# Turning the rows of x with a diagonal of 1/rms in the front of a hybrid decoder step

## The chip, the cores and the metric

The kernel runs on one core of a Trainium2 chip. The metric is the device time of one execution in microseconds, lower is better. All engines of the core work from one program: TensorE (PE, with its weight loads PEld), VectorE (DVE), ScalarE (ACT), GpSimd (POOL), and the SP queue, which issues most of the loads.

## What is computed

One layer of a decoder step over 1024 prompt rows and 64 sample rows of width 1024. Only the front of it is touched by the change: the adaLN coefficients, the normalised input h and the first columns of its large product.

```python
def rmsnorm(x, g):
    y = xf * lax.rsqrt(jnp.mean(xf * xf, axis=-1, keepdims=True) + EPS)
    return (y * g)
...
    mod = jax.nn.silu(c) @ w_ada + b_ada
    shift, scale, gate = jnp.split(mod, 3, axis=-1)
    h = rmsnorm(x, norm_g) * (1 + scale[:, None]) + shift[:, None]
    proj = h @ w_in
    u_pool, z_pool, z_ssm, xbc, dt_raw, g_raw = jnp.split(proj, SPLITS, axis=-1)
    ...
    y = (y + d_skip.astype(jnp.float32)[:, None] * xs).reshape(b, L, D_INNER)
```

The pooling branch, the convolution, the state-space scan, the output products and the final norm follow; their code is the same before and after.

## The kernel before

The activations are kept with channels on partitions and the 1088 rows along the free axis. x arrives the other way round, in nine blocks of rows (eight of 128, one of 64), so it is turned on TensorE. Products with h run with both operands split into a high and a low part (three matmuls for one), so each tile of h and of the weights is made twice: a rounded high part on ScalarE, and the rest by a subtraction on VectorE or GpSimd (`split`, L160 and L163, for weights; `h_make`, L307 and L299, for h).

`first()` writes the front out by hand, one call after the other, and `in_line` ties every instruction of each engine to this written order. The steps that matter:

- `x_load`, then `ada_load` (L253) and `w_load` (L852), are issued on the SP queue in the order in which they are wanted. A load that goes into a buffer in use waits on the SP queue for its last reader. `ada_load(2, 4..7)` goes into the buffers of part 1 of w_ada.
- `x_square` sums the squares of a block of rows on ScalarE or VectorE; `x_root` takes the square root on ScalarE; `x_unit` (L209, L215, L213) takes the reciprocal on VectorE and scales the rows in place.
- `x_turn(g3, k)` turns the 128 channels k of one of three groups of blocks (2, 3 and 4 blocks) by transposes (L226) into one PSUM tile, of which there are five in rotation, and copies it to `tf[k]` on VectorE (L232) or ScalarE (L230).
- `ada_mm(part, k)` (L261) multiplies silu(c) with one slice of w_ada; after eight of them `ada_out` copies the sum and `ada_end` turns it (L276) and makes the coefficients `md` (L280, L283) of a few channels. Part 0 serves channels k = 0, 1, part 1 k = 2, 3, part 2 k = 4 to 7.
- `h_make(g3, ks)` makes h of a group of rows, and `products` (L872 to L874) multiplies it with the first two weight tiles. `combine` (L490 to L492, L471) then forms sums of h for a Strassen-like scheme of seven products.
- `late_loads` is a generator: its first part loads conv_w, conv_b, dt_bias and d_skip; its second part spreads d_skip over 16 rows (`dx`, L366), turns conv's coefficients and `dx` on TensorE (L368, L369) and copies them out (L370, L371).
- `gate_mm` and `gate_end` (L838) make the gates' coefficients; then `run(wz, hook)` starts the seven products (L592 to L594), with the remaining weight splits (`first_steps`, L538) and sums between them.

Of the kernel before, what the change touches and what calls it, by code (L numbers as in the profile page):

```python
# [11 lines left out]
ALU = mybir.AluOpType  # L12
# [34 lines left out]
def tile_pool_ssd_step(  # L47
# [48 lines left out]
    def PB():  # L96
        return psB.tile([P, 512], F32, tag="ps", name=nm("ps"))
# [4 lines left out]
    def const(shape, name, dt=F32):  # L102
        return cp.tile(shape, dt, tag=name, name=name)
# [78 lines left out]
    xr = []  # L182
    xbig = [Y4(hs, F32), Y4(hs, F32)]
    ss = const([P, 9], "ss")
    rs = const([P, 9], "rs")
    hh_ = [None] * KT
    hl_ = [None] * KT

# [6 lines left out]
    def x_square(i, eng):  # L195
        xt, n = xr[i]
        sqj = pa.tile([P, D], F32, tag="rawA", name=nm("sqj"), bufs=3)
        if eng is V:
            V.scalar_tensor_tensor(sqj[:n], xt[:n], 1.0, xt[:n], ALU.mult, ALU.mult, accum_out=ss[:n, i:i + 1])
        else:  # L200
            act(sqj[:n], xt[:n], AF.Square, accum_out=ss[:n, i:i + 1])

    def x_root(a, b):
        n = xr[a][1]
        act(rs[:n, a:b], ss[:n, a:b], AF.Sqrt, bias=eps[:n], scale=1.0 / D)

    def x_unit(a, b):
        n = xr[a][1]
        V.reciprocal(rs[:n, a:b], rs[:n, a:b])  # L209
        for i in range(a, b):  # L210
            xt = xr[i][0][:n]
            if i == 6:
                act(xt, xt, AF.Copy, scale=rs[:n, i:i + 1])  # L213
            else:
                V.tensor_scalar(xt, xt, rs[:n, i:i + 1], None, ALU.mult)  # L215

    tf = [None] * KT

    def x_turn(g3, k, eng=None):
        if g3 == 0:  # L220
            tf[k] = tfp.tile([P, T], F32, tag="tf", name=nm("tf"), bufs=8)
        px = PB()
        c = 0
        for i in range((0, *XG)[g3], XG[g3]):
            xt, n = xr[i]
            nc.tensor.transpose(px[:, c:c + n], xt[:n, k * P:(k + 1) * P], ident[:n, :n])  # L226
            c += n
        o = BLK[g3][0]
        if eng is not V and (eng or k % 2):
            act(tf[k][:, o:o + c], px[:, :c], AF.Copy)  # L230
        else:
            V.tensor_copy(tf[k][:, o:o + c], px[:, :c])  # L232


    PARTS = ((0, 2), (2, 4), (4, 8))
# [120 lines left out]
    def late_loads():  # L356
        va = sm.tile([120, P], F32, tag="stc", name="va", bufs=4)
        load(va[0:96, :], conv_w[0].rearrange("k (m p) -> (k m) p", p=P))
        load(va[96:120, :], conv_b[0].rearrange("(m p) -> m p", p=P))
        V.memset(dtb, 0.0)  # L360
        load(dtb[0:NH, 0:1], dt_bias[0].rearrange("(h o) -> h o", o=1))
        dk = sm.tile([16, 2], F32, tag="rsm", name="dk")
        load(dk, d_skip[0].rearrange("(m h) -> m h", h=2))
        yield
        dx = sm.tile([16, 2, 64], F32, tag="stc", name="dx", bufs=4)
        V.tensor_copy(dx, dk.unsqueeze(2).to_broadcast([16, 2, 64]))  # L366
        ps = PB()
        nc.tensor.transpose(ps[:, :120], va, ident[:120, :120])  # L368
        nc.tensor.transpose(ps[:, 120:136], dx.rearrange("m h r -> m (h r)"), ident[:16, :16])  # L369
        V.tensor_copy(cvT, ps[:, :120])  # L370
        V.tensor_copy(Dv, ps[:, 120:136])  # L371
# [471 lines left out]
    def first():  # L843
# [56 lines left out]
        x_root(0, 2)  # L900
        x_unit(0, 2)
        x_square(2, None)
        x_square(3, None)
        x_root(2, 4)
        for k in range(4):
            x_turn(0, k, V)
        x_unit(2, 4)
        x_square(4, None)
        x_root(4, 5)
        for k in range(4, 8):  # L910
            x_turn(0, k)
# [56 lines left out]
        for k in range(4):  # L968
            ada_mm(2, k)
        products(2, range(2, 3))  # L970
        for k in range(4, 8):
            ada_mm(2, k)
        mr = ada_out(2)
        products(2, range(3, 4))
# [957 lines left out]
```

## Time and profile before

| what | value |
| --- | --- |
| median of the runs | 1312.61 us (1308.47, 1312.61, 1314.85) |
| the profiled execution | 1307.32 us, span 1305.6 us, granted clock 0.992 |
| PE / PEld busy | 1260.7 / 1164.8 us (97% / 89% of the span) |
| DVE, ACT, POOL busy | 887.2, 700.6, 677.9 us (68%, 54%, 52%) |
| chain that ended last | PE 79%, DVE 6%, DMA 6%, ACT 3%, issue 3%, POOL 2% |

The span runs from the first to the last instruction of the profiled execution; its own time has 1.7 us around that. A row of the timeline gives start and duration in us, engine, line, operation, output and inputs, how many alike follow each other (x), and in brackets how long the engine was idle before and what ended that. Matmuls are pipelined, so a row's duration includes the last one's drain. A row of the table by stage gives the stretch, its length, the busy time of PE, PEld, DVE, ACT and POOL with the number of instructions, the granted TensorE clock, the DMA engines' share and GB/s; asked for one line's instructions on one engine, it has only that engine's column. Lines such as L226 are those of the kernel before; in the changed kernel the same statements stand some ten lines lower.

### The profile page before, as it was taken

To read this page: it belongs to the slowest core of one execution; us is meant where nothing else is said; L and a number is where in the kernel's file an instruction comes from. 1 tells how busy PE (TensorE), PEld (TensorE's weight loads), DVE (VectorE), ACT (ScalarE), POOL (GpSimd) and SP (SyncE) were. 2 spreads that over 40 slices of the span, in tenths; PEclk is the share of its full clock that TensorE was granted. 3 is DMA by queue.
4 is the path that set the end of the run, shared out by engine and by line. 5 is a ranking of instruction groups with operands and counts; after the bars stand their busy time and mean duration, and the time that the engine had idled before them with its cause. 6 is when DMAs were issued, how large, how long until landed. Compare 5 with 4: busy or idle time off the path is not lost.

```text
span 1305.6 us, 26257 instructions
## 1 busy us (share of the span) xinstructions
PE 1260.7 (97%) x9667; PEld 1164.8 (89%) x9667; DVE 887.2 (68%) x1510; ACT 700.6 (54%) x1662; POOL 677.9 (52%) x562
## 2 busy tenths in 40 slices
PE   6889999999999999999999999999999999999998
PEld 4669999989999999999889999988888888999786
DVE  5677579966979587675657665487565877466533
ACT  6655347366557655555554554677887766201211
POOL 1005668678879777664344353366686756214000
PEclk9989999999999999999999999999999999999999
DMA  9726444465456453443546455999998665474621
GB/s 322 259 97 194 132 163 159 133 204 176 150 162 217 143 181 127 157 149 113 165 142 204 149 174 167 339 355 360 325 278 277 203 202 162 174 260 158 228 103 51
DMA packets 233794, 251.68 MB, mean 193 GB/s; under 512 B 31266, under 2 KB 177906, under 8 KB 233659
## 3 DMA queue, kind: packets, MB, share of 16 engines
q1 hardware_dynamic: 161568, 171.60, 41.0%
q10 hardware_dynamic: 72098, 78.41, 17.6%
q8 instruction: 77, 1.26, 0.4%
q14 instruction: 51, 0.41, 0.1%
HBM read 167.06 MB, written 83.01 MB: 192 GB/s over the span
## 4 chain that ended last, share of the span: by engine, by line
PE 79%; DVE 6%; DMA 6%; ACT 3%; issue 3%; POOL 2%; ACTq 0%; SPq 0%; DVEq 0%; POOLq 0%
PE ps L592 8%; PE mm L592 7%; PE ps L593 7%; PE ps L594 7%; PE mm L594 7%; PE mm L593 7%; PE mm L344 5%; PE mm L345 4%; PE mm L346 4%; PE ps L1878 2%; PE ps L1879 2%; PE ps L1880 2%; PE ps L1204 2%; PE ps L1420 1%; PE ps L1207 1%
## 5 line engine op out<-in xcount | busy, mean ns | idle before, releaser
L163 POOL TENSOR_TENSOR wlo<-rawA,whi 128x512 fp32r<-128x512 f32 x120 | 187.0, 1563 | 198.2 <-ACT whi L160 104.6
L163 POOL TENSOR_TENSOR wlo<-raw,whi 128x512 fp32r<-128x512 f32 x92 | 149.8, 1635 | 122.0 <-ACT whi L160 118.3
L344 PE MATMUL mm<-Y,whi 128*128 128x352 f32 (+1 forms) x480 | 164.0, 342 | 0.6 <-DVE G L1781 0.5
L345 PE MATMUL mm<-Y,whi 128*128 128x352 f32 (+1 forms) x480 | 158.1, 329 | 1.0 <-DVE Y L1455 1.0
L346 PE MATMUL mm<-Y,wlo 128*128 128x352 f32 (+1 forms) x480 | 157.5, 328 | 0.0
L594 PE MATMUL mm<-Y,wlo 128*128 128x272 f32 x496 | 144.1, 291 | 4.9 <-POOL wlo L163 4.4
L592 PE MATMUL mm<-Y,whi 128*128 128x272 f32 x496 | 146.9, 296 | 0.8 <-ACT whi L160 0.8
L592 PE MATMUL ps<-Y,whi 128*128 128x272 f32 x496 | 145.0, 292 | 2.1 <-ACT o L792 1.5
L593 PE MATMUL ps<-Y,whi 128*128 128x272 f32 x496 | 143.6, 290 | 0.0
L593 PE MATMUL mm<-Y,whi 128*128 128x272 f32 x496 | 143.4, 289 | 0.0
L594 PE MATMUL ps<-Y,wlo 128*128 128x272 f32 x496 | 143.1, 289 | 0.0
L160 ACT ACTIVATE whi<-rawA 128x512 fp32r<-128x512 f32 x125 | 78.2, 626 | 98.8 <-PE ps L593 45.5
L1047 DVE SCALAR_TENSOR_TENSOR GA<-GA,cvT,GA 128x1112 f32<-128x1112 f32 x72 | 127.1, 1769 | 1.8 <-ACT GA L1044 1.7
L160 ACT ACTIVATE whi<-raw 128x512 fp32r<-128x512 f32 x96 | 58.9, 626 | 90.0 <-DVE raw L538 39.0
L594 PEld LDWEIGHTS mm<-Y,wlo 128*128 128x128 f32 x496 | 94.0, 189 | 6.7 <-POOL wlo L163 5.7
L592 PEld LDWEIGHTS ps<-Y,whi 128*128 128x128 f32 x496 | 93.8, 189 | 3.8 <-ACT o L792 1.7
L344 PEld LDWEIGHTS mm<-Y,whi 128*128 128x128 f32 x480 | 90.7, 189 | 6.7 <-issue 3.9
L592 PEld LDWEIGHTS mm<-Y,whi 128*128 128x128 f32 x496 | 93.9, 189 | 2.6 <-ACT whi L160 1.0
L593 PEld LDWEIGHTS mm<-Y,whi 128*128 128x128 f32 x496 | 94.0, 189 | 0.7 <-issue 0.6
L593 PEld LDWEIGHTS ps<-Y,whi 128*128 128x128 f32 x496 | 93.9, 189 | 0.3 <-issue 0.2
L594 PEld LDWEIGHTS ps<-Y,wlo 128*128 128x128 f32 x496 | 93.9, 189 | 0.2 <-issue 0.2
L345 PEld LDWEIGHTS mm<-Y,whi 128*128 128x128 f32 x480 | 90.8, 189 | 1.7 <-DVE Y L1455 1.6
(446 smaller groups left out, 3778.7 us busy)
## 6 DMA issues: line engine op xcount, KB each, us to landing
rawA<-in_w_in SPq DMA_DIRECT2D x46, 512.0 KB
dec<-acs_d SPq DMA_DIRECT2D x32, 512.0 KB
xbc<-GA ACTq DMA_DIRECT2D x24, 512.0 KB
xb<-xbc SPq DMA_DIRECT2D x32, 384.0 KB
rawA<-in_w_in SPq DMA_DIRECT2D x32, 256.0 KB
pw<-in_w_ssm_out ACTq DMA_DIRECT2D x32, 256.0 KB
ws<-ph ACTq DMA_DIRECT2D x32, 256.0 KB
ws<-pw SPq DMA_DIRECT2D x32, 256.0 KB
```

The lines of the kernel that those rows point to most:

```text
L160: ins = act(hi[:, :, :ncols], raw[:, :, :ncols], AF.Copy)
L163: (eng or nc.gpsimd).tensor_tensor(lo[:, :, :ncols], raw[:, :, :ncols], hi[:, :, :ncols].bitcast(F32), ALU.subtract)
L344: mm(ps[:, :n], a, rh[k][:, o:o + n], start=(k == 0), stop=False)
L345: mm(ps[:, :n], a, rl[k][:, o:o + n], start=False, stop=False)
L346: mm(ps[:, :n], b, rh[k][:, o:o + n], start=False, stop=(k == nk - 1))
L592: mm(p, hi, ah, start=(k == 0), stop=False)
L593: mm(p, hi, al, start=False, stop=False)
L594: mm(p, lo, ah, start=False, stop=(k == 3))
L1047: V.scalar_tensor_tensor(d[:, :n], rp[:, k:k + n], cvT[:, 24 * k + mc:24 * k + mc + 1], d[:, :n], ALU.mult, ALU.add)
L1204: mm(o[hh], xd[:S, 2 * q + hh, :], dec[:S, 2 * q + hh], start=True, stop=state is None)
L1878: mm(ps[:, :cw], mhk, wo[k][0][:, s], start=(k == 0), stop=False)
L1879: mm(ps[:, :cw], mhk, wo[k][1][:, s], start=False, stop=False)
```

## The change

- `x_unit` no longer scales the rows. It builds, for every block of rows, a 128x128 diagonal matrix of 1/rms from the identity, in a tile `dg`. `x_turn` multiplies the raw rows with this diagonal in place of the transpose, which turns and scales at once.
- `x_turn` is split: the copy out of PSUM is a call of its own, `x_copy`, so that it can stand elsewhere in the written order; `x_turns` does both in a row, odd k on ScalarE, even k on VectorE.
- In `first()` the squares, roots and turns are written in another order: the squares of blocks 3 and 5 go from ScalarE to VectorE; roots and reciprocals are taken for blocks 2 to 4 and 5 to 8 together, in place of one to three at a time; four columns of the third group are turned ahead of the coefficient products of part 0; the last two columns are turned right behind the transposes of `ada_end(0)`, and their copies stand behind the first `products`.
- Four of the eight `ada_mm(1, k)` move from behind `products(1, ...)` and `h_make(2, ...)` to ahead of `products(1, ...)`.
- In `late_loads` a `yield` divides the second part: `dx` is made right after `combine` is set up, and the turning of conv's coefficients and `dx` comes after `gate_end`.
- `ss` is filled with ones at the start, since the root of blocks 5 to 8 now reads 128 rows of a block that has 64.

The order of the instructions that follow `first()` is the same on every engine.

```diff
     def x_unit(a, b):
         n = xr[a][1]
         V.reciprocal(rs[:n, a:b], rs[:n, a:b])
+        if not dg:
+            dg.append(R())
         for i in range(a, b):
-            xt = xr[i][0][:n]
-            if i == 6:
-                act(xt, xt, AF.Copy, scale=rs[:n, i:i + 1])
-            else:
-                V.tensor_scalar(xt, xt, rs[:n, i:i + 1], None, ALU.mult)
+            n = xr[i][1]
+            V.tensor_scalar(dg[0][:n, i * P:i * P + n], ident[:n, :n], rs[:n, i:i + 1], None, ALU.mult)
...
         for i in range((0, *XG)[g3], XG[g3]):
             xt, n = xr[i]
-            nc.tensor.transpose(px[:, c:c + n], xt[:n, k * P:(k + 1) * P], ident[:n, :n])
+            mm(px[:, c:c + n], xt[:n, k * P:(k + 1) * P], dg[0][:n, i * P:i * P + n], start=True, stop=True)
             c += n
+        return g3, k, px, c
+
+    def x_copy(turned, eng):
+        g3, k, px, c = turned
         o = BLK[g3][0]
-        if eng is not V and (eng or k % 2):
+        if eng is V:
+            V.tensor_copy(tf[k][:, o:o + c], px[:, :c])
+        else:
             act(tf[k][:, o:o + c], px[:, :c], AF.Copy)
-        else:
-            V.tensor_copy(tf[k][:, o:o + c], px[:, :c])
+
+    def x_turns(g3, ks):
+        for k in ks:
+            x_copy(x_turn(g3, k), nc.scalar if k % 2 else V)
...
         V.tensor_copy(dx, dk.unsqueeze(2).to_broadcast([16, 2, 64]))
+        yield
         ps = PB()
...
         x_unit(0, 2)
         x_square(2, None)
-        x_square(3, None)
-        x_root(2, 4)
-        for k in range(4):
-            x_turn(0, k, V)
-        x_unit(2, 4)
+        x_square(3, V)
+        x_turns(0, range(2))
         x_square(4, None)
-        x_root(4, 5)
-        for k in range(4, 8):
-            x_turn(0, k)
-        x_unit(4, 5)
-        x_square(5, None)
+        x_turns(0, range(2, 4))
+        x_root(2, 5)
+        x_unit(2, 5)
+        x_turns(0, range(4, 8))
+        x_square(5, V)
         x_square(6, None)
-        for k in range(4):
-            x_turn(1, k)
+        x_turns(1, range(4))
         x_square(7, V)
-        x_root(5, 8)
-        x_unit(5, 8)
         x_square(8, None)
-        x_root(8, 9)
-        for k in range(4, 8):
-            x_turn(1, k)
-        x_unit(8, 9)
+        x_turns(1, range(4, 6))
+        x_root(5, 9)
+        x_unit(5, 9)
+        x_turns(1, range(6, 8))
         v_turn()
-        for k in range(4):
+        x_turns(2, range(4))
+        for k in range(6):
             ada_mm(0, k)
-        x_turn(2, 0)
-        x_turn(2, 1)
-        ada_mm(0, 4)
-        ada_mm(0, 5)
+        x_turns(2, range(4, 5))
         w_split(0, 0)
         w_split(1, 0)
-        x_turn(2, 2)
-        x_turn(2, 3)
         ada_mm(0, 6)
         ada_mm(0, 7)
         mr = ada_out(0)
-        x_turn(2, 4, nc.scalar)
-        x_turn(2, 5, nc.scalar)
+        x_turns(2, range(5, 6))
         ada_end(0, mr)
+        turned = [x_turn(2, k) for k in (6, 7)]
         h_make(0, range(2))
         products(0, range(2))
-        x_turn(2, 6)
-        x_turn(2, 7)
+        x_copy(turned[0], V)
+        x_copy(turned[1], nc.scalar)
         h_make(1, range(2))
+        for k in range(4):
+            ada_mm(1, k)
         products(1, range(2))
         h_make(2, range(2))
-        for k in range(KT):
+        for k in range(4, KT):
             ada_mm(1, k)
...
         sums = combine()
+        next(late)
         for bi in range(3):
...
             gate_mm(k)
+        gate_end(bg)
         next(late, None)
-        gate_end(bg)
```

More of the change, by code (lines that the diff above doesn't have):

```diff
@@ L184, in tile_pool_ssd_step @@
     ss = const([P, 9], "ss")
+    nc.gpsimd.memset(ss, 1.0)
     rs = const([P, 9], "rs")
+    dg = []
     hh_ = [None] * KT
@@ L209, in x_unit, with x_turn @@
         V.reciprocal(rs[:n, a:b], rs[:n, a:b])
+        if not dg:
+            dg.append(R())
         for i in range(a, b):
-            xt = xr[i][0][:n]
-            if i == 6:
-                act(xt, xt, AF.Copy, scale=rs[:n, i:i + 1])
-            else:
-                V.tensor_scalar(xt, xt, rs[:n, i:i + 1], None, ALU.mult)
+            n = xr[i][1]
+            V.tensor_scalar(dg[0][:n, i * P:i * P + n], ident[:n, :n], rs[:n, i:i + 1], None, ALU.mult)
     tf = [None] * KT
-    def x_turn(g3, k, eng=None):
+    def x_turn(g3, k):
         if g3 == 0:
@@ L970, in first @@
         products(2, range(2, 3))
-        for k in range(4, 8):
+        for k in range(4, KT):
             ada_mm(2, k)
```

## The prediction

> **What bounds the kernel now.** I read the page first (busy shares, the slices), then tables by stage of the first 125 us, where every edited line runs, then the instructions of that stretch in order of time, one engine after the other, and last the rows near the end that already show the two new operations. The last stretch of the table by stage covers the rest.
>
> ```profile
> PE   6889999999999999999999999999999999999998
> ...
> 125.00:1305.00 1180.00, 1157.87 (x8805) 1079.79 (x8803) 804.68 (x1338) 626.05 (x1525) 656.89 (x520) 1.00 0.58 191
> ```
>
> The first number after the stretch's length is TensorE: from 125 us on it is busy 1157.87 of 1180 us. On every engine the written order of the instructions behind the edited stretch is the same before and after. So what the front wins, TensorE starts earlier with, and I let it pass to the end whole. In the first three slices TensorE is at 6 to 8 tenths; the edit lives in these holes.
>
> ```profile
> 9.62 3.67 PE L226 MATMUL ps<-ident,Y 128*128 128x128 f32 x16 [0.19 <-DVE Y L215]
> 21.05 1.08 PE L261 MATMUL ps<-Y,scT 128*32 128x128 f32 x32 [1.59 <-issue]
> 27.36 0.33 PE L276 MATMUL ps<-ident,mr 128*128 128x128 f32 x1
> 28.89 0.38 PE L872 MATMUL mm<-Y,whi 128*128 128x256 f32 x1 [1.20 <-ACT Y L307]
> 31.09 0.49 PE L226 MATMUL ps<-ident,Y 128*128 128x128 f32 x3
> 31.51 0.27 PE L226 MATMUL ps<-ident,R 64*128 64x64 f32 x1
> 31.71 0.55 PE L226 MATMUL ps<-ident,Y 128*128 128x128 f32 x3
> 33.69 0.45 PE L872 MATMUL mm<-Y,whi 128*128 128x384 f32 x1 [1.23 <-ACT Y L307]
> 37.67 2.56 PE L261 MATMUL ps<-G,scT 128*32 128x128 f32 x64
> 80.86 0.32 PE L368 MATMUL ps<-ident,va 120*128 120x120 f32 x1
> 84.76 0.29 PE L369 MATMUL ps<-ident,dx 16*128 16x16 f32 x1 [3.58 <-DVE dx L366]
> 84.98 0.60 PE L592 MATMUL mm<-Y,whi 128*128 128x272 f32 x1
> ...
> 90.41 0.29 PE L592 MATMUL mm<-G,whi 128*128 128x272 f32 x1
> 90.54 0.29 PE L593 MATMUL mm<-G,whi 128*128 128x272 f32 x1
> ```
>
> The bracket is the hole ahead of the row and who ended it. Three kinds stand here: waits in the turns of x; two waits of 1.2 us for the first rows of h (L872); and one of 3.58 us for a 16x128 copy (L366), behind which the first large product (L592) is queued.
>
> **Turning x by a product.** The row for a product of 32-bit 128x128 with a diagonal is in the trace, with the scaling of the identity that makes the diagonal:
>
> ```profile
> L226 PE MATMUL ps<-ident,Y x64: 270/421/476, 9.0 to 32.0; 128*128 128x128 f32 x64
> ...
> 15.00:18.20 3.20, 3.20 (x16) 1.00 1.09 262
> 18.45:19.10 0.65, 0.65 (x7) 1.00 1.09 344
> ...
> 1148.21 0.87 DVE L1734 TENSOR_SCALAR dg<-ident,rs 128x128 f32<-128x128 f32 x4
> 1153.41 1.05 PE L1735 MATMUL ps<-dg,ones 128*128 128x128 f32 x8
> ...
> 7.95 0.17 DVE L209 RECIPROCAL rs<-rs 128x2 f32<-128x2 f32 x1 [0.20 <-ACT rs L205]
> 8.15 1.42 DVE L215 TENSOR_SCALAR Y<-Y,rs 128x1024 f32<-128x1024 f32 x2
> ```
>
> The first row gives the shortest, median and longest time of one transpose in ns, the next two count the transposes (L226 alone) in two stretches. The 8 matmuls of L1735 are 4 calls: a product takes two passes. Leaving off the 0.27 us of the last one, a pass starts every (1.05 - 0.27)/7 = 0.11 us, so a product costs 0.22. A transpose is (0.49 - 0.27)/2 = 0.11 us at 31.09, and (3.67 - 0.42)/15 = 0.217 at 9.62, with the median 0.42 for the last. TensorE runs at half pace there: 16 transposes in 3.2 us from 15.0 on, 7 in 0.65 us after 18.45 (the clock column shows 1.00 for both; so early I go by the counts). So a product costs two transposes: 0.22 at full pace; at half pace no row shows it, and I take twice the half-pace transpose, 0.43. A chunk of 64 rows costs 0.20 (31.51 to 31.71) and becomes about 0.4.
>
> VectorE loses eight scalings of 0.7 us (L215) and ScalarE one; VectorE gets nine diagonals of 0.2 us (L1734: 0.87/4) and two squares more. TensorE can start when the reciprocal and one diagonal are done, 8.15 + 0.28 = 8.4, not 9.0, and then has no scaling to wait for: the 1.59 us at 21.05 (a copy out of PSUM queued behind scalings) goes. It runs without a break, so it should reach full pace after 3.4 to 6.9 us of work (before, the unbroken run from 15 on reached it at 18.4; the 3.7 us from 9.62 did not). Counting with the earlier one: 8 products at 0.43 to 11.9; 32 more of the first 40 at 0.22 to 18.9; 0.2 for L152; four columns of the third group (each 3 x 0.22 + 0.4) to 23.4; six steps of L261 at 0.27 (1.08/4) to 25.0; one column, two steps, one column to 27.7. That is where L276 now stands: 27.7 against 27.36, **+0.3**, and +2 with the late rise of pace. The copies moved between VectorE and ScalarE go at nothing: the lost scalings, some 5 us on VectorE, cover them; a copy without cover would cost TensorE about 0.4 to 0.6 us. The halves w_split makes move behind two copies on ScalarE; GpSimd's part has 1.5 us of room before L873 uses it:
>
> ```profile
> 24.75 2.50 POOL L163 TENSOR_TENSOR wlo<-raw,whi 128x512 fp32r<-128x512 f32 x2 [21.37 <-ACT whi L160]
> ```
>
> **Work put in the waits for h.** From 27.36 to the end of the coefficient products of part 1 (37.67 + 2.56 = 40.23) TensorE takes 12.9 us. After the change the last two columns of x (2.1 us as products) fill the 1.20 us ahead of 28.89, and four of the eight L261 steps (half of 2.56) fill the 1.23 us ahead of 33.69. What is left is work, the products with h at the pace of these two rows (0.17 us for 384 columns, so some 0.12 for 256):
>
> ```profile
> 45.16 0.34 PE L872 MATMUL mm<-Y,whi 128*128 128x384 f32 x1
> 45.33 0.34 PE L873 MATMUL mm<-Y,wlo 128*128 128x384 f32 x1
> ```
>
> 0.3 + 2.1 + 12 x 0.12 + 1.3 + 12 x 0.17 + 1.3 = 8.5 us. So part 1 ends at 27.7 + 8.5 = 36.2, **-4.0**.
>
> That does two things. First, the SP queue waits for exactly these steps, since part 2's last four loads reuse their buffers:
>
> ```profile
> 38.81 2.84 SPq L253 DMA_DIRECT2D G<-in_w_ada x4
> ...
> 36.00:39.00 3.00, 3.00 (x34) 2.47 (x36) 1.93 (x7) 1.75 (x3) 0.00 (x0) 0.50 0.23 64
> 39.00:41.50 2.50, 2.50 (x51) 2.17 (x44) 0.00 (x0) 0.28 (x1) 0.00 (x0) 1.00 0.65 192
> 41.50:47.50 6.00, 5.47 (x32) 4.50 (x30) 4.19 (x13) 3.72 (x7) 0.00 (x0) 1.00 1.05 325
> ```
>
> The last two columns are the DMA engines' share and GB/s: 0.23 and 0.65 before the loads arrive, full after. The hole is worth 0.77 x 3 + 0.35 x 2.5 = 3.2 us. With the first two loads free to go at about 32 and the last two by 36, I take 2.6 us of it as filled; the bounds are 0 and 3.2. Second, that hole decides what comes next:
>
> ```profile
> 51.75 0.69 DVE L538 TENSOR_TENSOR raw<-rawA,rawA 128x512 f32<-128x512 f32 x1 [0.73 <-DMA rawA<-in_w_in]
> ...
> 54.60 0.20 DVE L280 TENSOR_TENSOR md<-ps,vT 128x36 f32<-128x36 f32 x1 [1.43 <-PE ps L276]
> ```
>
> L538 waits for a load and the last coefficients (54.60) are queued behind it on VectorE. TensorE, 4 us ahead, no longer ends that wait; the load does: 51.75 - 2.6 = 49.1, plus L538 and the step behind it, 54.60 - 51.75 - 1.43 = 1.4, gives 50.6, **-4.0** for everything behind L280. Bounds: -1.4 (hole not filled) and -4.6. If TensorE is further ahead than VectorE there, it idles longer and may lose pace again; 0.5 us for that.
>
> **d_skip's rows.** L366 moves ahead of the sums of columns, so that its 16x128 copy is long done when TensorE reaches L369; it costs VectorE 0.21 us earlier. The 3.58 us wait goes whole. Next late would be the first weights; VectorE makes their low half just ahead of the row at 81.29:
>
> ```profile
> 81.29 0.69 DVE L538 TENSOR_TENSOR rawA<-raw,rawA 128x512 f32<-128x512 f32 x1
> 81.95 2.63 DVE L471 TENSOR_TENSOR Y<-tf,Y 128x544 fp32r<-128x544 f32 x4
> 84.50 0.21 DVE L366 COPY dx<-dk 16x128 f32<-16x128 f32 x1
> 85.36 0.41 DVE L838 TENSOR_TENSOR bg<-ps,bg 128x256 f32<-128x256 f32 x1
> 91.56 0.69 DVE L163 TENSOR_TENSOR wlo<-rawA,whi 128x512 fp32r<-128x512 f32 x1 [5.78 <-ACT whi L160]
> ...
> 85.00:90.70 5.70, 5.70 (x28) 5.70 (x28) 0.69 (x3) 0.48 (x2) 0.00 (x0) 0.55 0.06 13
> 91.50:114.40 22.90, 21.67 (x169) 21.01 (x167) 21.16 (x35) 14.59 (x30) 5.69 (x4) 1.00 0.38 119
> ```
>
> So L592 can start at 81.2 - 4.0 + 0.5 = 77.7 instead of 84.98. The clock column also says 0.55 behind the wait: the first 24 matmuls of L592 to L594 took 90.41 - 84.98 = 5.4 us, though at 90.41 the next starts after 0.13. Without the hole they take 24 x 0.13 = 3.1 and end at 80.8, 9.6 us earlier. That ending is what VectorE waited 5.78 us for (L163 behind ScalarE's L160, itself behind the copy of this product). VectorE's own list ends at 85.36 + 0.41 - 4.0 = 81.8, a little after, so its resumption at 91.56 becomes about 82.0: **-9.5**. From there to 114.4 VectorE is busy 21.16 of 22.90 us and sets the pace, so TensorE, now further ahead, wins nothing more; it will show small waits for it there.
>
> The Trainium skill ("TensorE: Matmul & The Clock Gate", Part 1) says one idle window of some 3.4 us halves the clock and a busy one restores it; by that the hole that I expect ahead of L280 (up to 3 us) would cost a whole window at half pace, 1.7 us instead of 0.5, and the sum would be -8.3. The trace is stricter than the rule: 0.55 behind the hole of 3.58 us, but also 0.50 from 36 to 39, behind one of 1.23 us and smaller ones.
>
> **Sum.** The +0.3 at L276 is in the -4.0 behind L280; then +0.5 for pace, -3.8 for the wait (84.98 to 81.2), -2.3 for the pace behind it, and 0.1 back for VectorE's list: -9.5. The profiled execution took 1307.32 us (span 1305.6 and 1.7 around it), so 1297.8 on its scale; it lies 5.3 below the median of the runs shown, 1312.61, and the forecast is set against that: 1312.61 - 9.5 = **1303.1**.
>
> **The rivals.**
> (a) VectorE takes the second half back: the DMA hole's gain arrives, but VectorE, or ScalarE's L160 in front of it, is late anyway, so only -4 to -6 is left: 1307.5. For it: from 81.29 to 84.7 VectorE's rows follow without a hole. Against: 5.78 us idle in the row of 91.56.
> (b) The loads do not move (SP issues them no earlier, or the DMA hole stays): the front gives about -1, d_skip's rows -6: 1306. Against it: the loads wait for L261 alone.
> (c) Slower: the product costs four transposes, not two, and the pace does not rise in the front. Deciding place: L276. Break-even is where the front's loss equals the rest of the gain, 9.5/60 = 0.16 us more per product than 0.22, that is 0.38. At 0.43 throughout (two passes at half pace) it is 60 x 0.21 = 12.6 less 9.8: +3, 1316. At four passes and half pace, 0.86, it is some 60 x 0.64 = 38 less 10: +28, 1341. Against: L1735 shows two passes, and the pace rose in the transposes. The Trainium skill (same page, Terms) calls transpose mode four times faster for 32-bit data, which speaks against this change: by it a product is 0.44 at full pace, 60 x 0.22 = 13 us lost, +3.5 in all. The trace's ratio is 2 (0.22 against 0.11).
> (d) It doesn't do what it says: the order inside the front is as written, but every piece is covered, since the DMA engines set the front all along: 1312. For it: full in 41.5 to 47.5. Against: 3.2 us of hole ahead of that.
>
> **How the numbers follow.** Forecast 0.60; (a) 0.14; (b) 0.08; (c) 0.12; (d) 0.06. The forecast's own bounds are -5.7 (DMA hole not filled, and 1.7 us of lost pace) and -10.6 (hole filled whole, no pace lost), 1302 to 1307; the runs shown spread some 3 us to either side, so 1299 to 1310. With (a) and (b), which 0.82 of the chance needs, the range is 1298 to 1311. Half a per cent (6.6 us) is about what a measurement of this kernel can tell from no change. Faster by more: 0.58 of the forecast's 0.60, 0.06 of (a), 0.04 of (b): 0.68. Within it: what is left of these, and (d): 0.20. Slower by more: (c), which I don't split, 0.12.
>
> **What would show it.** Right: L276 near 27 to 28; no hole ahead of L872's first rows over 0.5 us; the four L253 issues near 32 to 36; L280 near 50.6; no hole at L369, and a clock of 1.00 in the first product; VectorE's L163 near 82; the dense stretch of VectorE ending near 105 instead of 114.4. Wrong: two passes of over 0.25 us, L538 still at 51.7, or VectorE's hole of 5.78 us still open.

## The result, and the profile after

The changed kernel took 1299.05 us (median of 5 runs, 1296.04 to 1301.33) beside 1312.61 us for the kernel before (5 runs, 1308.47 to 1314.85): ratio 0.9902, 95% interval 0.9877 to 0.9928. Run again beside more runs of before, it took 1298.94 us (12 runs) against 1308.62 (28 runs): 0.9931, interval 0.9907 to 0.9954, or 9.0 us (6.0 to 12.2). It is faster. Here and below a gain in us is worked out from the ratio, which is estimated over all runs and is not quite the quotient of the two medians. The profiled execution took 1298.25 us, span 1296.5, against 1307.32 and 1305.6: 9.1 us less.

The stages of the profile after, in the order of the prediction. First TensorE's rows in order of time (start, duration, engine, line, operation, count, idle time before); lines stand some ten lower than before:

```profile
9.69 10.57 PE L228 MATMUL ps<-R,Y 128*128 128x128 f32 x80 [2.00 <-DVE R L216]
...
20.39 0.94 PE L228 MATMUL ps<-R,Y 128*128 128x128 f32 x6
21.25 0.43 PE L228 MATMUL ps<-R,R 64*128 64x64 f32 x2
21.61 0.94 PE L228 MATMUL ps<-R,Y 128*128 128x128 f32 x6
...
29.77 0.33 PE L286 MATMUL ps<-ident,mr 128*128 128x128 f32 x1
...
37.20 1.08 PE L271 MATMUL ps<-G,scT 128*32 128x128 f32 x32
...
79.16 0.23 PE L380 MATMUL ps<-ident,dx 16*128 16x16 f32 x1
79.32 0.40 PE L603 MATMUL mm<-Y,whi 128*128 128x272 f32 x1
...
82.46 0.29 PE L603 MATMUL mm<-G,whi 128*128 128x272 f32 x1
```

The turns of x run on without a hole; L286 (L276 before, at 27.36) is later by 2.4 us. The last coefficient products of part 1 end at 37.20 + 1.08 = 38.28, where they ended at 40.23. The hole of 3.58 us ahead of d_skip's rows is gone, and the first large product takes 82.46 - 79.32 = 3.1 us where it took 5.4. The counts of L228 alone in three stretches (length, TensorE busy with the number of matmuls), then all engines by stage (PE, PEld, DVE, ACT, POOL, clock, DMA share, GB/s):

```profile
9.69:12.60 2.91, 2.91 (x13) 1.00 1.03 411
13.00:16.00 3.00, 3.00 (x30) 1.00 1.06 262
...
30.00:36.00 6.00, 6.00 (x67) 5.29 (x67) 4.36 (x12) 4.55 (x8) 0.00 (x0) 1.00 1.06 351
36.00:41.50 5.50, 5.50 (x55) 4.30 (x53) 2.77 (x11) 3.16 (x7) 0.00 (x0) 1.00 1.00 326
41.50:53.00 11.50, 10.58 (x101) 7.41 (x100) 7.56 (x19) 5.66 (x10) 0.00 (x0) 1.00 0.98 321
84.00:105.50 21.50, 20.77 (x162) 20.12 (x161) 19.87 (x35) 13.74 (x28) 5.00 (x4) 1.00 0.40 126
125.00:1296.00 1171.00, 1149.12 (x8740) 1071.52 (x8738) 803.64 (x1330) 621.93 (x1516) 649.68 (x516) 1.00 0.59 190
```

13 passes in 2.91 us (0.22 each) and then 30 in 3.00: the pace rises at about 12.6, where it had not risen before 18.4. The loads run through from 30 to 53 (shares 0.98 to 1.06), and the half pace behind 36 us is gone. Then VectorE, the SP queue and ScalarE:

```profile
34.61 4.18 SPq L263 DMA_DIRECT2D G<-in_w_ada  x4
...
48.99 0.69 DVE L549 TENSOR_TENSOR raw<-rawA,rawA 128x512 f32<-128x512 f32 x1
...
52.65 0.20 DVE L290 TENSOR_TENSOR md<-ps,vT 128x36 f32<-128x36 f32 x1 [2.24 <-PE ps L286]
...
78.20 0.72 DVE L497 TENSOR_TENSOR Y<-tf,Y 128x544 fp32r<-128x544 f32 x1 [1.21 <-ACT Y L504]
...
84.00 0.68 DVE L163 TENSOR_TENSOR wlo<-rawA,whi 128x512 fp32r<-128x512 f32 x1
...
75.59 0.48 ACT L736 ACTIVATE dts<-mm,dtb 128x256 f32<-128x256 f32 x1 [1.33 <-DMA gs<-g]
```

The load behind L549 is there in time; md is now ended by TensorE (2.24 us), at 52.65 for 54.60. L163 starts at 84.00 without a wait, for 91.56 with one of 5.78. The two waits at 75 to 78 are new in size: ScalarE (L736) waits for the store gs<-g of the gates, 1.33 us for 0.15 before, and VectorE behind it, 1.21 for 0.50.

### The profile page after: what moved, and what is told of

Read it like the earlier page. It is cut to its first block, busy times and chain, and to the rows that moved or that the text cites. A ratio compares the mean times of both kernels' runs of the same rounds, so it can differ in the third digit from the quotient of the medians.

```text
span 1296.5 us, 26406 instructions
## 1 busy us (share of the span) xinstructions
PE 1261.6 (97%) x9739; PEld 1168.5 (90%) x9739; DVE 887.8 (68%) x1512; ACT 696.2 (54%) x1656; POOL 675.4 (52%) x563
## 3 DMA queue, kind: packets, MB, share of 16 engines
q8 instruction: 77, 1.26, 0.4%
## 5 line engine op out<-in xcount | busy, mean ns | idle before, releaser
L163 POOL TENSOR_TENSOR wlo<-rawA,whi 128x512 fp32r<-128x512 f32 x120 | 185.3, 1549 | 188.1 <-ACT whi L160 101.7
L163 POOL TENSOR_TENSOR wlo<-raw,whi 128x512 fp32r<-128x512 f32 x92 | 151.1, 1650 | 121.9 <-ACT whi L160 112.8
L603 PE MATMUL mm<-Y,whi 128*128 128x272 f32 x496 | 146.4, 295 | 0.2
L603 PE MATMUL ps<-Y,whi 128*128 128x272 f32 x496 | 144.4, 291 | 1.4 <-ACT o L803 1.4
L354 PEld LDWEIGHTS mm<-Y,whi 128*128 128x128 f32 x480 | 90.2, 188 | 6.9 <-issue 4.3
L603 PEld LDWEIGHTS ps<-Y,whi 128*128 128x128 f32 x496 | 93.3, 188 | 2.7 <-ACT o L803 1.6
L603 PEld LDWEIGHTS mm<-Y,whi 128*128 128x128 f32 x496 | 93.3, 188 | 2.3 <-issue 0.8
L604 PEld LDWEIGHTS mm<-Y,whi 128*128 128x128 f32 x496 | 93.4, 188 | 0.7 <-issue 0.6
L1196 ACT ACTIVATE dec<-dec,acT 128x128 f32<-128x128 f32 (+1 forms) x288 | 86.7, 383 | 10.0 <-POOL dec L1187 6.3
```

Of the source, the lines that this page charges most:

```text
L163: (eng or nc.gpsimd).tensor_tensor(lo[:, :, :ncols], raw[:, :, :ncols], hi[:, :, :ncols].bitcast(F32), ALU.subtract)
L354: mm(ps[:, :n], a, rh[k][:, o:o + n], start=(k == 0), stop=False)
L603: mm(p, hi, ah, start=(k == 0), stop=False)
L604: mm(p, hi, al, start=False, stop=False)
L1196: act(dec[:, h], dec[:, h], AF.Exp, bias=acT[:S, c, 8 * g + h:8 * g + h + 1], scale=-1.0)
```

## The experiments

### The two parts apart: d_skip's rows, and the front

d_skip alone, on the kernel before:

```diff
         V.tensor_copy(dx, dk.unsqueeze(2).to_broadcast([16, 2, 64]))
+        yield
...
         sums = combine()
+        next(late)
...
-        next(late, None)
         gate_end(bg)
+        next(late, None)
```

> The kernel before with only one part of the change: the step that turns d_skip's rows is cut in two, its VectorE copy runs ahead of the loop over the gate's products and its two transposes come after them, behind gate_end. Front of the kernel untouched. Theory A (the two terms of 53 to 92 us stand by themselves): md stays at 54.6, the second transpose no longer waits 3.58 us for VectorE, so that the products of L592 start at about 81.4 instead of 84.98; with no hole there is no window of half pace, the first product takes 3.1 us instead of 5.4, the first L163 starts near 85.7 instead of 91.56, and the kernel is 5 to 6 us faster (ratio about 0.9955). Theory B (VectorE takes it back, since it is dense from 91.5 to 114.4): L592 starts at 81.4 but VectorE's last step of that stretch moves by less than 2 us, gain 0 to 2 us.

The front alone is the changed kernel with these three places put back.

> The changed kernel with that one part undone: d_skip's rows stand where they stood before, the products with diagonals and the new order of the front stay. Theory A: md starts at 52.6 as in the changed kernel (1.95 us ahead of before), the hole of about 3.6 us before the second transpose and the window of half pace behind it are back, the first L163 starts near 89.6, and the kernel is 2 us faster than before (1.5 to 3 with the even pace of the front). Theory B (the front carries most of the gain, since the pace rises earlier for good): 5 us or more faster.

Measured: d_skip alone 1304.37 us beside 1309.08 (10 and 31 runs), ratio 0.9972 (0.9952 to 0.9991), 3.7 us; the front alone 1305.9, ratio 0.9965 (0.9944 to 0.9987), 4.6 us. Together 8.3, beside 9.0 for the whole: they add up, as far as intervals of 1.2 to 6.3 and 1.7 to 7.3 us can tell. TensorE's and VectorE's rows of d_skip alone, and its stages:

```profile
84.03 0.23 PE L370 MATMUL ps<-ident,dx 16*128 16x16 f32 x1
84.19 0.40 PE L593 MATMUL mm<-Y,whi 128*128 128x272 f32 x1
```

```profile
88.47 0.69 DVE L163 TENSOR_TENSOR wlo<-rawA,whi 128x512 fp32r<-128x512 f32 x1 [1.32 <-ACT whi L160]
```

```profile
27.40:56.00 28.60, 24.93 (x215) 18.98 (x213) 14.55 (x38) 13.72 (x25) 0.40 (x2) 0.88 0.84 280
84.10:91.00 6.90, 6.90 (x55) 6.87 (x56) 5.58 (x12) 5.29 (x10) 0.00 (x0) 1.00 0.09 24
```

The wait and the half pace behind it are gone, as theory A has it (55 matmuls in 6.9 us at clock 1.00, where before had 34 in 6.5 at 0.60). But its front, which is the same code as before, stood at a clock of 0.88 from 27 to 56, where the profiled execution of before had 0.94, and md came at 56.01, not 54.60. From md to L163 it takes 32.46 us, where before took 36.96: 4.5 us won, of the 5 to 6 expected. In that stretch stands a window at half pace, 60.0 to 63.4 (clock 0.50), which the profiled execution of before does not have. The timed 3.7 us (1.2 to 6.3) lies between the two theories and decides neither. The front alone:

```profile
53.50 0.20 DVE L290 TENSOR_TENSOR md<-ps,vT 128x36 f32<-128x36 f32 x1 [2.25 <-PE ps L286]
...
79.59 0.73 DVE L496 TENSOR_TENSOR Y<-tf,Y 128x544 fp32r<-128x544 f32 x1 [1.87 <-ACT Y L503]
...
91.38 0.69 DVE L163 TENSOR_TENSOR wlo<-rawA,whi 128x512 fp32r<-128x512 f32 x1 [5.34 <-ACT whi L160]
```

In this trace md is 1.1 us ahead of the profiled before, 2.5 ahead of the trace above, and 1.4 us is lost again on the wait for gs (1.87 where before had 0.50), so that L163 stands where it stood. The trace thus gives less than the timed 4.6 us (1.7 to 7.3); the time lies between the two theories and decides neither.

### Half pace: filling the holes of before with idle work

```diff
         nc.tensor.transpose(ps[:, :120], va, ident[:120, :120])
+        for _ in range(30):
+            nc.tensor.transpose(ps[:, 136:264], ident, ident)
         nc.tensor.transpose(ps[:, 120:136], dx.rearrange("m h r -> m (h r)"), ident[:16, :16])
```

> The kernel before with 30 extra transposes of the identity, into columns that nobody reads, between the two transposes of d_skip's step: TensorE's hole of 3.58 us before the second one is filled with about 30 x 0.11 = 3.3 us of idle work, and nothing is moved. It leaves the wait where it was and takes away only the idle. Theory A (the half pace of 83.35 to 90.18 comes from the hole): the clock stays at 1.00 through 83 to 92, the first product takes 3.1 us instead of 5.4, L592 still starts near 85, the first L163 near 89.3, the kernel is 2 us faster. Theory B (the pace falls for another reason, the load itself): the clock shows 0.5 again, no gain, or a loss of up to 0.5.

TensorE's rows of it in order of time, and the stage behind them:

```profile
83.20 3.44 PE L370 MATMUL ps<-ident 128*128 128x128 f32 x30
86.64 0.23 PE L371 MATMUL ps<-ident,dx 16*128 16x16 f32 x1
86.80 0.40 PE L594 MATMUL mm<-Y,whi 128*128 128x272 f32 x1
```

```profile
86.80:92.00 5.20, 5.20 (x42) 5.20 (x42) 1.61 (x5) 2.26 (x5) 0.00 (x0) 1.00 0.05 11
```

42 matmuls in 5.2 us at 1.00, behind the same wait: the half pace there comes from the hole, and is worth the 2.3 us of the prediction (the first 24 take 3.1 us, 86.80 to 89.94, where they took 5.4). The other traces agree: a half-paced window follows in all four that have this hole (3.17 to 4.94 us long), and in none of the nine that do not. In time it is 0.9996 (0.9972 to 1.0020), which holds both the 2 us (0.9985) and nothing: the runs scatter by more than this term (1302.99 to 1315.78 us). So the next one puts idle transposes at four holes of the front, on the kernel before, and leaves this one open:

```diff
+        if g3 == 1 and k == 0:                       # x_turn, ahead of the transposes
+            for _ in range(9):
+                nc.tensor.transpose(px[:, 384:512], ident, ident)
...
+            if part == 0:                            # ada_mm, ahead of the first product
+                for _ in range(12):
+                    nc.tensor.transpose(pm[part][:, 256:384], ident, ident)
...
+        if part != 1:                                # ada_end, behind its transposes
+            for _ in range(8):
+                nc.tensor.transpose(pm[part][:, 256:384], ident, ident)
```

> The kernel before with its front's holes filled by idle transposes of the identity: 9 ahead of the second group of rows (hole of 1.05 us), 12 ahead of the first coefficient product (1.59), 8 each ahead of the first products of L872 (1.20) and of the last set (1.26). Nothing moved, the hole of 3.58 us before d_skip's rows left in. Theory A (before's half-paced windows at 20 to 60 us come from these holes, so that they fall otherwise in every execution): no half pace between the rise and 80 us, mean granted clock about 0.992 to 0.993 against before's 0.989, md at 53.5 to 55, the kernel 2 to 3 us faster than before. Theory B (other cause): windows as before, no gain, or up to 1.5 us slower for the idle work.

1307.81 us beside 1308.77 (12 and 17 runs), ratio 0.9983 (0.9964 to 1.0001), 2.2 us with an interval that reaches nothing. The mean granted clock of its runs is 0.993, before's 0.989. Its rows show that two of the four holes stayed open:

```profile
14.77 2.62 PE L229 MATMUL ps<-ident,Y 128*128 128x128 f32 x22 [1.06 <-DVE Y L215]
...
20.06 1.53 PE L265 MATMUL ps<-ident 128*128 128x128 f32 x12 [2.49 <-DVE tf L235]
```

The nine idle transposes ran at 12.34, ahead of two transposes of x that were not late, and the hole came behind these. The twelve waited for VectorE's copy out of PSUM (L235) themselves, and their 1.5 us came on top of that wait. The other two holes shrank, from 1.20 to 0.33 us and from 1.26 to 0.38. md came at 54.97, for 54.60 before. So the run does not tell what filling the whole front is worth. No half pace followed the hole of 2.49 us; one window was left, behind a hole of 1.23 us at the second L872 that had no filler. The stage with that hole, and the window behind it:

```profile
27.70:35.80 8.10, 5.66 (x35) 4.29 (x35) 3.77 (x10) 4.71 (x9) 0.19 (x1) 1.00 1.02 346
35.80:39.30 3.50, 3.50 (x33) 2.98 (x35) 2.52 (x9) 1.75 (x3) 0.00 (x0) 0.51 0.06 15
```

### Four coefficient products moved, alone

```diff
+        for k in range(4):
+            ada_mm(1, k)
         products(1, range(2))
         h_make(2, range(2))
-        for k in range(KT):
+        for k in range(4, KT):
             ada_mm(1, k)
```

> The kernel before with only four of the eight coefficient products of the second set moved ahead of products(1), so that the sync queue's four loads of L253 are issued at 32 to 36 us instead of 38.81. Theory A (the hole of 3.2 us in the loads sets part of the front): the transfers run through 35 to 39, md starts 1 to 2 us ahead of 54.60, the kernel is 1 to 2 us faster. Theory B (the loads are hidden, TensorE's order sets md): the transfers move, md does not move by more than 0.3, no change in time. Theory C (as the prediction had it, the loads and the hole are the larger part of 4 us): md 3 us or more earlier.

Measured: 1307.43 us (10 runs), ratio 0.9988 (0.9969 to 1.0006), and a trace that cannot decide: TensorE was at half pace from 21.5 to 38.5 us, L276 came at 30.65, md at 57.51, and SP's loads at 38.81 as before, though 3.3 us nearer to L276. A stage of it:

```profile
31.00:38.50 7.50, 6.18 (x37) 4.82 (x40) 2.33 (x7) 2.66 (x6) 0.00 (x0) 0.50 0.81 271
```

### The changed kernel once more, its late start, and its order without the product

> The changed kernel itself, timed beside the three kernels below. Before's front showed half-paced windows at other places in each of the last executions, the changed kernel's none up to 613 us. Theory A (a good part of the gain is pace: windows of 3.41 us at half pace that before's holes let in by chance and the changed kernel has no holes for): mean granted clock 0.996 to 0.997 against before's 0.989, no half pace before 125 us in the profile, ratio to before 0.991 to 0.994, spread smaller than before's. Theory B (the gain is the 9 us of the front's marks alone and the clock no part of it): clocks of both alike within 0.002, ratio 0.993.

The time is the one told above, 1298.94 us at a ratio of 0.9931. Mean granted clock 0.996 in its 12 runs, 0.989 in 76 runs of before. Among those 76, the 17 with a clock up to 0.986 have a median of 1312.77 us, the 19 from 0.992 up 1305.96. So pace goes with how before's runs scatter. The two groups lie 0.008 of clock and 6.8 us apart; at that rate the 0.0064 between the two kernels' clocks (0.9957 and 0.9893) would be some 5 of the 9 us. That is an estimate and not shown, since a wait that lowers the clock also costs time by itself. Theory A's marks are there: no half pace before 125 us in the profile, and a ratio of 0.9931.

The profile after shows the first product late, and the table load of the square root late ahead of it. That row in before, then both rows after:

```profile
6.33 1.28 ACT L205 ACT_TABLE_LOAD   x1
```

```profile
7.53 1.28 ACT L207 ACT_TABLE_LOAD   x1 [0.93 <-DVE sqj L201]
8.82 0.29 ACT L207 ACTIVATE rs<-ss,eps 128x2 f32<-128x2 f32 x1
```

In before, the table load of the square root starts at 6.33 without a wait, under the squares. With `ss` filled by GpSimd the root depends on two engines, the fill on GpSimd and the squares (sqj), and its table load now waits for the squares. That the load carries one of the root's two waits is a reading of this row. The experiment fills `ss` on VectorE:

```diff
-    nc.gpsimd.memset(ss, 1.0)
+    V.memset(ss, 1.0)
```

> The changed kernel with ss set by VectorE instead of GpSimd. The square root then waits for one engine, not for two, and its table load for none. Theory A (that wait made the front 1.2 us late): the table load of L207 starts at 6.3 to 6.6 instead of 7.53, the first product of L228 at about 8.5 instead of 9.69, L286 at 28.6 instead of 29.77, and the kernel is about 1.2 us faster than the changed kernel. Theory B (the loads bind from 30 us on, the DMA engines being full from 30 to 50): L286 earlier, md at L290 unmoved at 52.65, no gain. Theory C: row 0 of x lands as late as the table load ends, L228 moves by 0.3 only.

Its rows on ScalarE and on TensorE, and the counts of L228 in two stretches:

```profile
6.30 1.28 ACT L207 ACT_TABLE_LOAD   x1
```

```profile
8.47 11.88 PE L228 MATMUL ps<-R,Y 128*128 128x128 f32 x80 [1.09 <-DVE R L216]
29.85 0.33 PE L286 MATMUL ps<-ident,mr 128*128 128x128 f32 x1
```

```profile
8.47:14.10 5.63, 5.63 (x26) 1.00 1.03 377
14.10:17.10 3.00, 3.00 (x29) 1.00 1.09 319
```

The wait is shown as its cause: the load starts at 6.30, the first product at 8.47, the 1.2 us that were expected. They did not arrive at L286 (29.85) in this trace, for a reason that none of the three theories had: the pace rose only at 14.1 us, and 26 passes ran at half pace instead of 13. The time does not show them either (1299.36 us, ratio 0.9927, 0.9898 to 0.9956). This trace also has a half-paced window from 55.1 to 58.5 us, behind a hole of 1.25 us ahead of the products that wait for md; the changed kernel's two traces have the same hole (1.25 us each) and no window there.

The order without the product:

```diff
-            V.tensor_scalar(dg[0][:n, i * P:i * P + n], ident[:n, :n], rs[:n, i:i + 1], None, ALU.mult)
+            xt = xr[i][0][:n]
+            if i == 6:
+                act(xt, xt, AF.Copy, scale=rs[:n, i:i + 1])
+            else:
+                V.tensor_scalar(xt, xt, rs[:n, i:i + 1], None, ALU.mult)
...
-            mm(px[:, c:c + n], xt[:n, k * P:(k + 1) * P], dg[0][:n, i * P:i * P + n], start=True, stop=True)
+            nc.tensor.transpose(px[:, c:c + n], xt[:n, k * P:(k + 1) * P], ident[:n, :n])
```

> The changed kernel's order with the rows scaled and transposed as before (on VectorE, tile 6 on ScalarE), without a product. Theory A (the product is worth more than it costs, since it keeps TensorE busy from 9.7 us on): holes of 1 us and more come back before L286, the clock shows half pace somewhere in 12 to 50 us, L286 starts at 28 to 30 and md at 53 to 55, the kernel is 1 to 3 us slower than the changed kernel. Theory B (the order alone does it, the product only costs TensorE 72 x 0.11 = 7.9 us): L286 at 26 to 28, the kernel 1 to 3 us faster than the changed kernel.

Two stages of it:

```profile
12.00:21.50 9.50, 6.17 (x37) 4.65 (x35) 8.37 (x18) 7.04 (x16) 0.00 (x0) 1.00 1.10 308
21.70:28.50 6.80, 6.62 (x63) 4.57 (x62) 2.53 (x6) 2.21 (x5) 1.19 (x1) 0.50 1.10 350
```

Holes are back (6.17 us busy of 9.5), half pace behind them, and md at 53.17; mean clock 0.9925 in 12 runs. The coefficients' transposes of part 0 start at 30.62, where 28 to 30 was expected. For the rest this is theory A's picture, but in time 1300.19 us, ratio 0.9942 (0.9917 to 0.9966), 1.25 us behind the changed kernel and not told apart from it. The order and d_skip's rows carry most of the gain; what the product adds is within the scatter.

### A rule for the front, and versions built on it

In the four traces with products that had been taken by then, L286 starts 18.6 us after the first product plus half of the time until the pace rises (a fit, good to 0.05 us). That gives a price to idle work ahead of the first product. On top of the fill by VectorE:

```diff
         ps = PB()                                    # c_turn
+        for _ in range(24):
+            nc.tensor.transpose(ps[:, 128:256], ident, ident)
...
         px = PB()                                    # x_turn
+        if g3 == 0 and k == 0:
+            for _ in range(6):
+                nc.tensor.transpose(px[:, 384:512], ident, ident)
```

> e3_ss_vector with idle transposes of the identity into unread columns: 24 ahead of the first transposes of c (TensorE is idle there up to 6.4 us) and 6 between those and the first product. In the four traces of the order with products, L286 starts at the first product + 18.6 us + half of the time from the first product to the rise of the pace (9.69, 12.61 -> 29.77; 9.85, 13.45 -> 30.25; 9.74, 14.36 -> 30.63; 8.47, 14.12 -> 29.85): TensorE bound, at half pace until the rise. Theory A (that is the rule): the pace has risen by the first product at about 8.5 to 9.2, L286 starts at 27.1 to 28.0 instead of 29.77, md at 50 to 51 instead of 52.65, the kernel is 1.5 to 2.5 us faster than the changed kernel. Theory B (the pace rises only with the real load, or the loads bind from 30 us): the rise stays at 12 to 15 or md stays at 52 to 52.7, no gain.

TensorE's rows of it:

```profile
1.61 5.38 PE L147 MATMUL ps<-ident 128*128 128x128 f32 x24 [1.61 <-POOL ident masks.py:199]
7.79 0.88 PE L230 MATMUL ps<-ident 128*128 128x128 f32 x6
8.64 9.30 PE L233 MATMUL ps<-R,Y 128*128 128x128 f32 x80
...
27.80 0.33 PE L291 MATMUL ps<-ident,mr 128*128 128x128 f32 x1
```

1295.54 us, ratio 0.9885 (0.9860 to 0.9911), 3.4 us below the changed kernel's other runs, though the two intervals still touch. The pace rises amid the idle transposes (24 at 0.22 us, 6 at 0.12), the 80 passes take 9.30 us where they took 10.57, L291 starts at 27.80 (the rule: 8.64 + 18.6 = 27.2), md at 50.67: theory A. The third group of rows offers a second step: scaled and transposed it costs half the passes, while VectorE and ScalarE idle.

```diff
+            if i >= 5:                               # x_unit, ahead of the diagonal
+                xt = xr[i][0][:n]
+                if i % 2:
+                    V.tensor_scalar(xt, xt, rs[:n, i:i + 1], None, ALU.mult)
+                else:
+                    act(xt, xt, AF.Copy, scale=rs[:n, i:i + 1])
+                continue
...
+            if g3 == 2:                              # x_turn, ahead of the product
+                nc.tensor.transpose(px[:, c:c + n], xt[:n, k * P:(k + 1) * P], ident[:n, :n])
+                c += n
+                continue
...
-        x_turns(2, range(4))
-        for k in range(6):
+        for k in range(4):
+            ada_mm(0, k)
+        x_turns(2, range(4))
+        for k in range(4, 6):
             ada_mm(0, k)
```

> e3_ss_vector with the third group of rows (tiles 5 to 8) scaled, two on VectorE and two on ScalarE, and transposed, the first two groups by products, and four of the coefficient products ahead of the third group. TensorE is without a gap from 9.7 us to 53.86 in the changed kernel; this takes 32 x 0.11 = 3.5 us of its work away while VectorE and ScalarE idle. Theory A (TensorE sets the front): L286 near 25, md near 49, kernel 4 to 5 us faster than the changed kernel. Theory B (the loads set it, DMA engines being full from 30 to 50): holes at TensorE behind L286, waiting for DMA, md at 51 to 52.6, kernel 0 to 1.5 us faster, with a half-paced window where a hole is 1 us or more perhaps slower.

Its rows on VectorE around md, on TensorE behind md, and the stage after that:

```profile
49.79 0.69 DVE L560 TENSOR_TENSOR raw<-raw,rawA 128x512 f32<-128x512 f32 x1
50.40 0.19 DVE L301 TENSOR_TENSOR md<-ps,vT 128x36 f32<-128x36 f32 x1
```

```profile
51.60 0.38 PE L894 MATMUL mm<-G,whi 128*128 128x256 f32 x1 [1.91 <-ACT G L328]
```

```profile
53.30:56.70 3.40, 2.93 (x14) 2.70 (x13) 2.45 (x6) 3.33 (x6) 0.00 (x0) 0.50 0.48 175
```

The coefficients' transposes of part 0 start 3.1 us earlier than in the changed kernel (26.66), md 2.25 us earlier (50.40), delayed by VectorE's L560 just ahead of it; then come a hole of 1.91 us and a window at half pace, and L603's counterpart starts only 1.05 us earlier (78.27). 1298.28 us, ratio 0.9921 (0.9893 to 0.9950): no gain over the changed kernel that can be told, of the 4 to 5 us of theory A. The last version has both steps, and 8 idle transposes behind the transposes of part 2, in the hole:

```diff
+        if part == 2:                                # ada_end
+            for _ in range(8):
+                nc.tensor.transpose(pm[part][:, 256:384], ident, ident)
```

> e7_group2 with the same idle transposes ahead of the first product, and 8 more behind the last transposes of L286 into a bank that has been read, which fill 0.9 us of the hole of 1.9 us ahead of the products that wait for md. Theory A (TensorE and its pace still set the front): L286 near 25.3 (26.66 in e7_group2, where 3.0 us at half pace cost 1.5), no half pace at 53 to 57, md at 49 to 50.4, the products of L592 near 76, the kernel 2 to 3 us faster than e7_group2. Theory B (the loads, or VectorE, which held md by 0.7 us there, set the front by now): L286 earlier but md within 0.5 of 50.4, gain under 1 us.

TensorE's row of slices on its page, and one stage:

```profile
PE   9999999999999999999999999999999989999997
```

```profile
53.00:79.30 26.30, 26.30 (x254) 18.90 (x253) 23.27 (x45) 19.29 (x35) 0.00 (x0) 1.00 0.45 152
```

In the slices there is no digit under 9 in the front, where before had 688; idle transposes count as busy there. In 53 to 79 us TensorE has no hole left, and clock 1.00. md at 48.42, L603's counterpart at 75.08. 1293.62 us beside 1308.77 (6 and 17 runs), ratio 0.9872 (0.9847 to 0.9897): the lowest median of all versions. It was not timed in one comparison with the others, but its interval lies clear of the changed kernel's repeat (0.9907 to 0.9954), though not of its first comparison (0.9877 to 0.9928); its six runs, 1289.05 to 1296.52 us, lie below 14 of the changed kernel's 17. The 4.7 us below the version without the idle work are more than the 2 to 3 expected.

## Why the prediction came out as it did

1303.1 us was forecast, within 1298 to 1311; 1299.05 was measured. The change of 9.5 us was worked out on the profiled execution of before, and the profiled pair shows 9.1. Most of what lies between 1303.1 and 1299.05 is the scale: the first five runs of before had a median of 1312.61, the 31, 28 and 17 of the later comparisons 1309.08, 1308.62 and 1308.77, while the changed kernel repeated at 1298.94. The agreement of 9.5 with 9.1 is closer than its steps, and so in part luck:

| step | forecast | profile after |
| --- | --- | --- |
| first product | 8.4 | 9.69 |
| L276/L286 | 27.7 (+0.3) | 29.77 (+2.4) |
| from there to the end of part 1's coefficient products | 8.5 | 8.51 (before 12.87) |
| L538/L549 | 49.1 | 48.99 |
| md, L280/L290 | 50.6 (-4.0) | 52.65 (-1.95) |
| first large product starts | 77.7 | 79.32 (-5.7) |
| its 24 matmuls | 3.1 | 3.1 (before 5.4) |
| L163 | 82.0 (-9.5) | 84.00 (-7.6) |
| end of VectorE's dense stretch | 105 | 106.2 (-8.2) |

At L163 the change had won 1.9 us less than forecast. Behind it the forecast has nothing more to win, but 0.6 us came by the end of the dense stretch and 0.9 by the end of the kernel, in code that is the same; why is open.

**The mis-sized term is the +0.3 at L276.** Of the 2.07 us that it came later than forecast, 1.29 is the start, since the wait on the table load was not seen (shown by filling `ss` on VectorE: 8.47, though L286 did not follow there). The first 40 products took 10.57 us, for 10.5 forecast, so the half pace was rightly counted. The rest is in the columns of the third group: 21.61 - 20.39 = 1.22 us each, not 1.06, since six passes of 128 rows take 0.86 and not 0.66 there; why is not settled. The steps between them took a little less than forecast. The four loads were issued from 34.61 to 38.79 us, for 38.81 to 41.65 before and a forecast of 32 to 36. L549 came as forecast (48.99 for 49.1), but with TensorE 2 us late it was TensorE, not the load, that ended the wait for md.

**Work in the waits for h, d_skip's rows, the pace behind them:** right. 8.51 us for 8.5, no hole at L380, clock 1.00 in the first product; the filler showed that the hole alone makes that half pace.

**What came back later.** From md to the first large product 26.67 us are left of 30.38, 3.7 less; the 3.8 for the wait. VectorE gave 0.7 us back on the wait for gs, a little of rival (a), and its list ended at 83.39 + 0.41, not at 81.8: the 2.0 us by which md was late. The 0.5 us for lost pace behind md did not come: the hole there is 1.25 us, as long as before (1.26), and the clock is 1.00 from 53.4 to 60.0. Rivals (b) and (d) fall with the rows of the loads and of TensorE. Rival (c) too: 40 products took 10.57 us, some of them at half pace, so two passes each. The Trainium skill ("TensorE: Matmul & The Clock Gate", Terms) has transpose mode four times faster for 32-bit data; these rows disagree, the factor is two.

**What the forecast did not have** is that before's front is not one number. Half-paced windows stand at other places of it in every execution (35.6 us; 29.3 and 36.1; 20.4, 30.6 and 37.4), and with the same code md came at 54.60, 56.01 and 56.78 us in these three traces. In four traces with the products and the new order it came at 52.65 to 53.50. On these means the front is worth 2.8 us, not the 1.95 of the profiled pair. Not all of the scatter is the front's: behind 600 us, in code that is the same, each of the thirteen traces has one to four such windows of 3.41 us ahead of the last one (673.9 and 1148.3 us in before, 613.4 and 668.0 in the changed kernel). How much of the 9 us is pace rather than waits is open: the runs' clocks suggest that a good part is, and the idle transposes at four of the front's holes, which filled two, gave 2.2 us with an interval down to nothing.

## What to carry to other kernels

Where the tensor engine has short waits at the front, a single profile is one draw of where the half-paced windows fall; compare the granted clock of all runs before pricing a stage from one. Idle transposes into unread columns, ahead of the first real work and in holes that cannot be closed, cost nothing where the engine waits anyway, if they do not wait for the same thing as the work behind them; twelve that did left the hole open and came on top of it. Ahead of the first work they are worth 3.4 us in the medians here, and the product 1.25 over scaling; neither is clear of the noise by itself. An added fill on a second engine can put a wait on an instruction that used to start early, such as a table load: look at what the first instructions wait for, not only at how long they take.

## What the runs showed of the hardware

Transposes alone raise the pace: 24 of the identity from 1.61 us on at 0.22 us each, and the passes behind them at 0.116. The Trainium skill ("TensorE: Matmul & The Clock Gate", Part 4) says that the full clock does not engage for transpose mode; the trace disagrees, by these numbers.

Without idle transposes ahead of it, the rise comes at 12.3 to 14.4 us for first products at 8.5 to 9.9, so 2.9 to 5.6 us after them. The Trainium skill (same page, Part 1) has a free-running window of 3.4 us that does not start with the kernel; the traces agree in that the earliest start, 8.47, had one of the latest rises, 14.1. The Trainium skill (same page, "Why this matters for your kernels") also advises against idle gaps of over some 3 us; here a hole of 1.91 us with smaller ones beside it (0.41 and 0.47) was followed by a window at 0.50, so the measurement is the stricter one.

Whether a hole of this size brings a window is not the same in every trace. A hole of 1.25 or 1.26 us stands ahead of the products that wait for md in ten traces, and a half-paced window began within 3 us of it in three of them. Ahead of the first coefficient product, holes of 2.53 us were followed by one in two traces, and the hole of 2.49 us in a third was not.
